# A two-layer decoder trunk on one core: work moved to GpSimd, and layer two's first key blocks begun on the first tokens

## The chip, the cores and the metric

The kernel runs on one core of a Trainium2 chip. Its engines are TensorE (PE in the profile; PEld is its weight load), VectorE (DVE), ScalarE (ACT), GpSimd (POOL) and SyncE (SP), which here only issues the transfers from memory. Every engine works through its own instructions in order, and they wait for each other with semaphores. The metric is the device time of one execution in microseconds (us), lower is better. 0.2% of it, about 1.25 us, is what a comparison of runs can tell from no change.

## What is computed

256 tokens of 1024 features pass two layers. Each layer has an attention part with two kinds of heads and a squared-ReLU MLP, and each part is wrapped in normalizations before and after.

```python
for l in range(DEPTH):                       # 2
    h = _rms_norm(x, g_pre_mix[l])
    parts = jnp.split(h @ w_in[l], split_at, axis=-1)
    o_nsa = _nsa_mixer(...)                  # 8 query heads, 2 key/value heads, head size 64
    o_fox = _fox_mixer(...)                  # 8 heads, forgetting attention
    mix = jnp.concatenate([o_nsa, o_fox], axis=-1) @ w_out[l]
    x = x + _rms_norm(mix, g_post_mix[l])
    h = _rms_norm(x, g_pre_mlp[l])
    y = jnp.square(jax.nn.relu(h @ w_up[l])) @ w_down[l]
    x = x + _rms_norm(y, g_post_mlp[l])
```

An NSA head has three branches, mixed with learned gates: attention over compressed blocks, over selected blocks, and over a window. With 256 tokens the selection takes every block and the window every earlier token, so branches 1 and 2 are two causal attentions over different keys and values. The compressed branch joins 32 tokens of keys (or values) into one vector, sends it through a small network with a GELU, and so gets 15 compressed keys and values. Keys and queries of the other branches are rotated by position (the first 16 of 64 features). A FoX head is causal attention with a bias from cumulated forget gates.

## The kernel before

**Numbers as pairs.** To reach float32 accuracy with TensorE's fast format, each operand is split into a high part (ACT copies it, rounded: `whi`, and the halves of `xT`, `qS`, `kx`, `oT`, `aT`) and the rest (DVE subtracts: `wlo`). Every product becomes three: high-high, high-low, low-high. So every weight tile costs one ACT and one DVE instruction, 1024 columns each (`Weights.get`, L621).

**Stages of a layer.** (1) The input projection. One chunk (chunk 1) has tokens as rows and holds the values and gates; 16 blocks of 128 columns have tokens as columns (`block`, L1225): 0 and 1 are the keys of branches 1 and 2 (`kT`), 2 and 3 the raw keys and values for compression (`cT`), 4 to 7 NSA queries, 8 to 15 FoX queries and keys. (2) Attention, spread over the rest of the projection, which fills PE between the small steps (`fill`, L1293). (3) The output projection, then `sandwich` (L856): normalize, add to x, and make the next transposed operand `xT`. (4) The MLP, eight chunks of `up` and `down`, then again `sandwich`.

**Turn into layer two.** In layer two chunk 1 goes token half by token half (`in_chunk` with `by_token`, L1127): all products for tokens 0 to 127, and only then those for 128 to 255, so that the first can run while the second half's `sandwich` is still at work. Its last steps (transposes into `xT`, then `m` and the update of x) are called inside that loop (L1445 to L1450). Then come blocks 0, 1, 2 and so on; each adds up in one of the two `acc` banks of PSUM over all 256 tokens: eight 512-column products with `whi` (high and low half of xT at once) and eight 256-column ones with `wlo`. The two `acc` banks first hold the MLP sums of the second token half, and `m` reads them last.

**Rotation.** `turned` (L972) multiplies by a sine table (`m`), shuffles partitions, multiplies the source by a cosine table (`y`), adds, and splits. It runs three times a layer: for the keys, and for two pairs of query blocks. The tables carry the row normalization (`row_scales`, L1249).

**Gather for compression.** `gather_blocks` (L982) lays the raw keys or values out for the compressing network in `kstk` and `kstv`: eight copies of 64 partitions x 120 elements each, from key head g and position parity j, and one copy of the position vector. Where g equals j the copy stays in its own partitions, otherwise it goes to the other half of them. For keys all eight are on ACT, for values all eight on DVE.

**One attention element.** There are 24 in a layer: NSA pair x parity x branch (16) and FoX pair x parity (8). Scores on PE; DVE adds the mask and takes the row minimum (`pr`, `st`); ACT takes the exponential with row sums; DVE the reciprocal; then `scale` (L1358) multiplies the two pieces of the probabilities (128 and 256 columns) by the reciprocal and the gate: NSA branch 1 on ACT, NSA branch 2 and FoX on DVE. PE then turns the three 128-column pieces (`probs_T`, L1374), ACT copies them out, and they are multiplied with the values later. The loop (L1483) scales element i-1 beside the scores of i, and turns i-2.

**Order.** The program first records every operation (`Recorder`), and then works out one fixed order for each engine (`order`, L483): it lays the operations out with a table of prices (`_cost`, L576, and `_latency`, L562), derives due times, and tries 140 slightly shifted rankings. So a change of a price or an engine changes the order everywhere, and PE's order on the chip is fixed. Before the change the recorder knows tensor, vector, scalar and sync; GpSimd has no part.

Of the kernel before, what the change touches and what calls it, by code (L numbers as in the profile page):

```python
# [24 lines left out]
P = 128  # L25
# [198 lines left out]
class Recorder:  # L224
    def __init__(self, nc, tc):
        self.nc, self.tc = nc, tc
        self.ops, self.fifo, self.key, self.hot, self.lane, self.group = [], {}, None, False, None, None
        self.after, self.cuts = None, []
        for e in ("tensor", "vector", "scalar", "sync"):
            setattr(self, e, _Engine(self, e))  # L230

    def tile(self, pool, shape, dtype, name, tag=None, bufs=1, psum=False):
# [69 lines left out]
    def schedule(self, rank):  # L302
# [9 lines left out]
        for op in self.ops:  # L312
            op.missing, op.ready, op.start = len(op.deps), 0.0, None
            for b in op.bufs:
                left[b] = b.ops
        waiting = {e: [] for e in ("tensor", "vector", "scalar", "sync")}
        busy = dict.fromkeys(waiting, 0.0)
        bus, last, sent = 0.0, None, 0
        busy["sync"] = 730.0
# [124 lines left out]
    def trial(self, out, seed):  # L444


        rng = np.random.default_rng(seed)
        late = rng.exponential(LATE[seed % 2], len(self.ops))
        ends, left = {}, {b: b.ops for q in self.fifo.values() for b in q}
        slots = {tag: [None] * q[0].bufs for tag, q in self.fifo.items()}  # L450
        free = dict(tensor=0.0, vector=0.0, scalar=0.0, sync=730.0)
        bus, last, sent, gone, reach = 0.0, None, 0, {}, [0.0] * (len(self.cuts) + 1)
        for n, op in enumerate(out):
            t = free[op.engine]
            for d, lat in op.deps.items():
                t = max(t, ends[d] + lat)
            for b in op.bufs:
                if left[b] == b.ops:
                    ring = slots[b.tag]
                    x, i = min((gone[p] if p else 0.0, i) for i, p in enumerate(ring) if p is None or not left[p])  # L460
                    ring[i] = b
                    t = max(t, x)
            if op.engine == "sync":
                free["sync"] = t + 470
                sent += 1
                bus = max(bus, t + 1150) + op.cost * (1.0 if t > CALM else EARLY) + (THIRD if sent == 3 else 0)
                ends[op] = bus + 900 + (late[n] if t > CALM else 0)
            else:
                ends[op] = t + op.cost
                if op.engine == "tensor":  # L470
                    ends[op] += _turn(last, op)
                    last = op
                    reach[op.stage] = max(reach[op.stage], ends[op])
                elif t > CALM:
                    ends[op] += FEW
                free[op.engine] = ends[op]
            for b in op.bufs:
                left[b] -= 1
                gone[b] = max(gone.get(b, 0.0), ends[op] + (260 if b.psum else 150))
        reach[-1] = max(ends.values())  # L480
        return np.diff([0.0] + reach)
# [80 lines left out]
def _latency(a, b):  # L562
    if a.engine == "sync":
        return 50.0
    if a.engine == b.engine == "tensor":
        return 0.0
    if a.engine == "tensor":
        return 40.0 + (360.0 if b.name == "tensor_tensor_reduce" else 200.0)
    if b.engine == "tensor":
        return 100.0 + (260.0 if a.engine == "vector" else 230.0)  # L570
    if a.engine == b.engine:
        return 190.0 if a.engine == "vector" else 225.0
    return 40.0 + (130.0 if a.engine == "vector" else 145.0)


def _cost(op, views):  # L576
    out = op.args[0] if op.args else op.kw["out"]
    n = int(np.prod(out.shape[1:]))
    if op.engine == "sync":
        v = views[0][1]  # L580
        return v.shape[0] * int(np.prod(v.shape[1:])) * 4 / 320.0
    if op.engine == "tensor":
        if op.name == "stretch":
            if op.args[2][0][0] == "transpose":
                return 108.0 * len(op.args[2])

            tiles = [_shape(x[1][1]) for x in op.args[2]]
            return sum((x[1][0].ix.size / (2.4 if x[1][1].dtype == F32R else 0.6) + 20) / (P // min(t))
                       for x, t in zip(op.args[2], tiles)) + RETILE * sum(a != b for a, b in zip(tiles, tiles[1:]))
        if op.name == "transpose":  # L590
            return 83.0 if op.args[1].dtype == F32R else 108.0
        if op.args[1].dtype == F32R:
            return 13.6 + n / 2.4
        return max(220.0, 3 + n / 0.6)
    if op.engine == "vector":
        if op.name == "reciprocal":
            return 60 + 6.5 * n
        if op.name == "tensor_reduce":
            n = int(np.prod(op.args[1].shape[1:]))
        fast = op.name in ("tensor_copy", "tensor_scalar", "memset") and not any(v.buf.psum for _, v in views)  # L600
        aps = sum(isinstance(v, View) for v in op.args[2:4]) if op.name == "tensor_scalar" else int(
            op.name == "scalar_tensor_tensor" and isinstance(op.args[2], View))
        return 68 + 64 * aps + n * (0.52 if fast else 1.04) + 10 * (op.name == "tensor_tensor_reduce")
    src = op.args[1]
    aps = sum(isinstance(op.kw.get(k), View) for k in ("bias", "scale", "accum_out"))
    return n / 1.2 + (55 if src.buf.psum else 92) + 93 * aps
# [54 lines left out]
def trunk(nc, A, consts_in, out, sbp, pp):  # L661
# [260 lines left out]
    for l in range(DEPTH):  # L922
# [49 lines left out]
        def turned(src, hi, lo):  # L972
# [2 lines left out]
            y = tokt("y").rearrange("p (b n) -> p b n", b=2)  # L975
            nc.vector.tensor_mul(m, src, two(T["rS"]))
            nc.vector.stream_shuffle(m, m, TURNED)
            nc.vector.tensor_mul(y, src, two(T["rC"]))
            nc.vector.tensor_add(y, y, m)
            split(y, (hi, lo))  # L980

        def gather_blocks(si):  # L982
# [4 lines left out]
            for g in range(2):  # L987
                rows = slice(g * HD, g * HD + HD)
                for j in range(2):
                    h = slice(j * HD, j * HD + HD)  # L990
                    for i in (0, 8):
                        o, x = kst[s][h, i:i + 8, g, 0:15], src[rows, :, i // 8:i // 8 + 15, j]
                        if si:
                            nc.vector.tensor_copy(o, x)
                        else:
                            nc.scalar.activation(o, x, AF.Copy)
            nc.vector.tensor_copy(kst[s][:, :, :, 15:16], posT[s][:, :, None, None].to_broadcast([P, 16, 2, 1]))

        def hidden_part(s, q):
            if q == 0:  # L1000
# [123 lines left out]
            T["cum"] = cum  # L1124


        def in_chunk(c, evac, by_token=False):  # L1127
            n = columns(l, c)[1] - columns(l, c)[0]
            parts = parts_of(l, c)
            begin = len(nc.ops)  # L1130
            ps = [None, None]
            ws = {}

            def piece(t, k, hi, lo, k0):
                if k == 0:
                    ps[t] = psum("os"[t] if first else "ox"[t] if by_token else "acc")
                mm3(ps[t][:, :n], [y[:, k, t * P:t * P + P] for y in xT[:2]], (hi[:, k - k0, :], lo[:, k - k0, :]),
                    k == 0, k == 7)

            if by_token:  # L1140
                for t in range(NT):
                    for q, (k0, k1) in enumerate(parts):
                        if t == 0:
                            ws[q] = weight(l, "in", c, q)
                        for k in range(k0, k1):
                            piece(t, k, *ws[q], k0)
                            yield
                    evac(t, ps[t])
                    yield
                return  # L1150
            for q, (k0, k1) in enumerate(parts):
                w = weight(l, "in", c, q)
                for k in range(k0, k1):
                    for t in range(NT):
                        piece(t, k, *w, k0)
                        yield
            nc.key = begin if EVKEY else None
            for t in range(NT):
                evac(t, ps[t])
            nc.key = None  # L1160
            yield

        def block_home(b):

# [108 lines left out]
        def stream():  # L1273
            def part(name, gen):
                yield from gen
                done.add(name)
            for b in range(4 if first else 0, NB):
                yield from part(b, block(b))
            yield from part("c5", in_chunk(5, evac5))
            for k in range(LASTK):  # L1280
# [77 lines left out]
        def scale(e, p, st):  # L1358
            kind, pair, par, br = e[:4]
            nc.vector.reciprocal(st[:, 2:4], st[:, 2:4])  # L1360
            for a, b, t in SEGS:
                if kind == "fox":
                    nc.vector.tensor_scalar(p[:, a:b], p[:, a:b], st[:, 2 + t:3 + t], None, op0=OP.mult)
                elif br == 1:
                    c = 3 * (2 * pair + par) + br
                    if t == 0:
# [1 line left out]
                    nc.scalar.activation(p[:, a:b], p[:, a:b], AF.Copy, scale=st[:, 2 + t:3 + t])  # L1368
                else:
                    c = 3 * (2 * pair + par) + br  # L1370
                    nc.vector.tensor_scalar(p[:, a:b], p[:, a:b], st[:, 2 + t:3 + t], gate[t][:, c:c + 1],
                                            op0=OP.mult, op1=OP.mult)

        def probs_T(*es):  # L1374
# [67 lines left out]
                        r_mix[t] = rstd_of_x(t, "rm")  # L1442
        else:

            for n, _ in enumerate(in_chunk(1, evac1, by_token=True)):  # L1445
                if n == 6:
                    urgent(carry)
                    next(carry)
# [1 line left out]
                        r_mix[t] = rstd_of_x(t, "rm")  # L1450
        if first:
            nc.scalar.activation(selr, cst[:, C_SEL:C_SEL + 8], AF.Copy)
        else:
            fill_to(1)
        row_scales()
        kx = [tile([P, 2, S], F32R, name="kx", tag=f"kx{j}") for j in range(2)]
        posT = {"k": rows[:, 0:16], "v": rows[:, 16:32]}
# [256 lines left out]
```

## Time and profile before

| | |
|---|---|
| time, median of 3 runs | 623.85 us (623.78 to 624.29) |
| the profiled execution, its own time | 623.83 us |
| its span, first to last instruction | 622.1 us |
| TensorE (PE) busy | 609.5 us, 98% |
| VectorE (DVE) busy | 475.0 us, 76% |
| ScalarE (ACT) busy | 389.9 us, 63% |
| GpSimd (POOL) busy | 0.2 us |

In the profile a row of a group names line, engine, operation, tiles (out<-in), shape and count, then busy time and the mean of one in ns, and after the second bar the idle time ahead and what ended it. Nearly all rows have line L535, the helper that emits the recorded operations, so they are told apart by tile and shape. A timeline row has start, length, engine and group, and in brackets the idle time before it. Matmuls overlap and their ends are modelled, so intervals from start to start say more than their lengths. A window row has busy time of PE, PEld, DVE, ACT and POOL in turn, then TensorE's clock, and the transfers.

### The profile page before, as it was taken

How to read it: one execution, taken by the hardware profiler on the slowest of the kernel's cores; microseconds unless marked ns; L12 is line 12 of the kernel's file. 1: busy time of each engine (PE TensorE's matmuls, PEld its weight loads, DVE VectorE, ACT ScalarE, POOL GpSimd, SP SyncE). 2: the span in 40 equal slices, each digit the busy share in tenths (PEclk: the TensorE clock that was granted, in tenths of full speed). 3: DMA queues.
4: the chain of work that ended last, by engine and by line, in shares of the span. 5: the costliest groups of instructions: out<-in, count | busy, mean ns of one | idle time of the engine just before them, and what ended most of it. 6: DMA issues, size and time to landing. Idle time of an engine off the chain costs nothing.

```text
span 622.1 us, 9781 instructions
## 1 busy us (share of the span) xinstructions
PE 609.5 (98%) x3472; PEld 505.2 (81%) x3472; DVE 475.0 (76%) x1057; ACT 389.9 (63%) x802; POOL 0.2 (0%) x4
## 2 busy tenths in 40 slices
PE   9999999999999999999999999999999999999995
PEld 8877777778888888888878778878888888888884
DVE  6889997789976566566599999996997666566544
ACT  6869796667655455455476588975766555556422
POOL 0000000000000000000000000000000000000000
PEclk9999999999999999999999999999999999999998
DMA  8967865219766556555427645552486556555101
GB/s 296 402 236 260 298 192 171 102 35 290 251 192 205 181 187 201 189 180 191 136 81 245 244 136 213 202 179 67 166 273 205 177 195 202 192 181 204 34 1 68
DMA packets 36353, 115.98 MB, mean 186 GB/s; under 512 B 4432, under 2 KB 6224, under 8 KB 36304
## 3 DMA queue, kind: packets, MB, share of 16 engines
q1 hardware_dynamic: 36304, 115.36, 54.7%
q8 instruction: 27, 0.44, 0.3%
q14 instruction: 22, 0.18, 0.1%
HBM read 114.30 MB, written 1.05 MB: 185 GB/s over the span
## 4 chain that ended last, share of the span: by engine, by line
PE 86%; DVE 8%; ACT 4%; issue 1%; DVEq 0%
PE s L535 34%; PE acc L535 25%; PE x L535 20%; PE o L535 7%; DVE wlo L535 2%; ACT pr L535 1%; DVE m L535 1%; ACT kstk L535 1%; ACT whi L535 1%; DVE y L535 1%; DVE pr L535 1%; DVE kstv L535 0%; DVE mg L535 0%; DVE qT L535 0%; ACT rl L535 0%
## 5 line engine op out<-in xcount | busy, mean ns | idle before, releaser
L535 DVE TENSOR_TENSOR wlo<-wraw,whi 128x1024 fp32r<-128x1024 f32 (+2 forms) x200 | 230.6, 1159 | 91.6 <-ACT whi L535 91.0
L535 ACT ACTIVATE whi<-wraw 128x1024 fp32r<-128x1024 f32 (+3 forms) x200 | 199.8, 1006 | 121.6 <-PE acc L535 58.6
L535 PE MATMUL s<-xT,whi 128*128 128x512 f32 x448 | 111.9, 392 | 0.0
L535 PEld LDWEIGHTS s<-xT,whi 128*128 128x128 f32 x448 | 81.4, 189 | 15.1
L535 PE MATMUL acc<-whi,aT 128*128 128x512 f32 x256 | 88.5, 390 | 0.0
L535 PE MATMUL x<-whi,aT 128*128 128x512 f32 x256 | 88.4, 390 | 0.0
L535 PE MATMUL acc<-xT,whi 128*128 128x512 f32 (+1 forms) x242 | 66.3, 400 | 0.3 <-DVE qT L535 0.3
L535 PEld LDWEIGHTS s<-xT,wlo 128*128 128x128 f32 x448 | 61.1, 190 | 4.4
L535 PE MATMUL s<-xT,wlo 128*128 128x256 f32 x448 | 62.5, 282 | 0.0
L535 ACT ACTIVATE pr<-pr,st 128x128 f32<-128x128 f32 (+1 forms) x128 | 55.1, 448 | 9.4 <-DVE st L535 9.3
L535 PEld LDWEIGHTS acc<-whi,aT 128*128 128x128 f32 x256 | 48.0, 188 | 10.0
L535 PEld LDWEIGHTS x<-whi,aT 128*128 128x128 f32 x256 | 48.1, 188 | 9.7
L535 PEld LDWEIGHTS acc<-xT,whi 128*128 128x128 f32 x242 | 43.1, 191 | 9.6 <-issue 1.1
L535 PE MATMUL x<-wlo,aT 128*128 128x512 f32 x128 | 50.0, 390 | 0.0
L535 PE MATMUL acc<-wlo,aT 128*128 128x512 f32 x128 | 49.9, 390 | 0.0
L535 PE MATMUL acc<-xT,wlo 128*128 128x256 f32 x240 | 37.1, 285 | 0.5 <-DVE wlo L535 0.5
L535 PEld LDWEIGHTS acc<-xT,wlo 128*128 128x128 f32 x240 | 33.6, 189 | 3.4 <-DVE wlo L535 0.9
L535 ACT ACTIVATE rl<-h 128x512 f32<-128x512 f32 x28 | 17.5, 624 | 18.7 <-DVE h L535 18.7
L535 PEld LDWEIGHTS acc<-wlo,aT 128*128 128x128 f32 x128 | 24.0, 188 | 4.9
L535 PEld LDWEIGHTS x<-wlo,aT 128*128 128x128 f32 x128 | 24.1, 188 | 4.5
L535 ACT ACTIVATE rl<-x 128x512 f32<-128x512 f32 x24 | 14.7, 612 | 20.1 <-PE x L535 16.0
L535 PE MATMUL o<-whi,xT 128*128 128x512 f32 (+1 forms) x80 | 26.1, 377 | 0.0
(224 smaller groups left out, 865.9 us busy)
## 6 DMA issues: line engine op xcount, KB each, us to landing
wraw<-in_w_up_dram SPq DMA_DIRECT2D x64, 512.0 KB, 4.2
wraw<-in_w_down_dram SPq DMA_DIRECT2D x64, 512.0 KB, 3.3
wraw<-in_w_fm_dram SPq DMA_DIRECT2D x28, 512.0 KB, 5.0
wraw<-in_w_out_dram SPq DMA_DIRECT2D x16, 512.0 KB, 6.6
wraw<-in_w_dram SPq DMA_DIRECT2D x9, 512.0 KB, 3.6
w<-in_cmp_w_k_dram SPq DMA_DIRECT2D x8, 512.0 KB, 5.6
w<-in_cmp_w_v_dram SPq DMA_DIRECT2D x8, 512.0 KB, 3.8
wraw<-in_w_dram SPq DMA_DIRECT2D x6, 256.0 KB, 4.2
```

The costliest lines, as they stand in the source:

```text
L535: getattr(getattr(self.nc, op.engine), name)(*[real(v) for v in args], **{k: real(v) for k, v in kw.items()})
```

## The change

- `scale`: the two multiplications of NSA branch 2 and of FoX go from DVE to GpSimd (64 instructions over both layers). NSA branch 1 stays on ACT.
- `gather_blocks`: copies with g equal to j (four of eight, "straight down" in their own partitions) go to GpSimd, the four others to ACT, for keys and values alike; the position copies go from DVE to GpSimd.
- `turned`: the multiplication with the cosine table goes from DVE to GpSimd.
- Layer two: a new generator `by_token` replaces the option of `in_chunk`. After the products of token half 0 it begins blocks 0 and 1 for those tokens (`half_block`, eight 256-column products with `whi` each), then does token half 1 of chunk 1, then the second halves of the two blocks and their `wlo` products. The stream of the other blocks starts at 2.
- The recorder and its layout get GpSimd as an engine, with prices of its own.

```diff
-        for e in ("tensor", "vector", "scalar", "sync"):
+        for e in ("tensor", "vector", "scalar", "gpsimd", "sync"):
...
+    if "gpsimd" in (a.engine, b.engine):
+        return 260.0
...
+    if op.engine == "gpsimd":
+        return 160 + n * (2.2 if op.name.startswith("tensor_tensor") or op.name == "tensor_mul" else 1.0)
...
             nc.vector.stream_shuffle(m, m, TURNED)
-            nc.vector.tensor_mul(y, src, two(T["rC"]))
+            nc.gpsimd.tensor_mul(y, src, two(T["rC"]))
...
-                        if si:
-                            nc.vector.tensor_copy(o, x)
+                        if g == j:
+                            nc.gpsimd.tensor_copy(o, x)
                         else:
                             nc.scalar.activation(o, x, AF.Copy)
-            nc.vector.tensor_copy(kst[s][:, :, :, 15:16], posT[s][:, :, None, None].to_broadcast([P, 16, 2, 1]))
+            nc.gpsimd.tensor_copy(kst[s][:, :, :, 15:16], posT[s][:, :, None, None].to_broadcast([P, 16, 2, 1]))
...
+        def by_token():
+            n = columns(l, 1)[1] - columns(l, 1)[0]
+            ws, wb, pb, homes = {}, {}, {}, {}
+
+            def tokens(t):
+                ps = psum("ox"[t])
+                for q, (k0, k1) in enumerate(parts_of(l, 1)):
+                    if t == 0:
+                        ws[q] = weight(l, "in", 1, q)
+                    for k in range(k0, k1):
+                        piece(t, k, ps[:, :n], *ws[q], k0)
+                        yield
+                evac1(t, ps)
+                yield
+
+            def half_block(b, t):
+                o = pb[b].rearrange("p (j n) -> p j n", j=2)[:, :, t * P:t * P + P]
+                for k in range(8):
+                    nc.tensor.matmul(o, wb[b][0][:, k, :], xT[2][:, k, :, t * P:t * P + P], start=t == 0 and k == 0,
+                                     stop=False, skip_group_check=True)
+                    if k % 2:
+                        yield
+
+            yield from tokens(0)
+            for b in range(2):
+                homes[b] = block_home(b)
+                wb[b] = weight(l, "in", "b", b)
+                pb[b] = psum("acc")
+                yield from half_block(b, 0)
+            yield from tokens(1)
+            for b in range(2):
+                yield from half_block(b, 1)
+                for k in range(8):
+                    nc.tensor.matmul(pb[b][:, S:], wb[b][1][:, k, :], xT[0][:, k, :], start=False, stop=k == 7,
+                                     skip_group_check=True)
+                    if k % 2:
+                        yield
+                both_halves(homes[b], pb[b])
+                yield
...
-            for b in range(4 if first else 0, NB):
+            for b in range(4 if first else 2, NB):
...
                 if kind == "fox":
-                    nc.vector.tensor_scalar(p[:, a:b], p[:, a:b], st[:, 2 + t:3 + t], None, op0=OP.mult)
+                    nc.gpsimd.tensor_scalar(p[:, a:b], p[:, a:b], st[:, 2 + t:3 + t], None, op0=OP.mult)
...
-                    nc.vector.tensor_scalar(p[:, a:b], p[:, a:b], st[:, 2 + t:3 + t], gate[t][:, c:c + 1],
+                    nc.gpsimd.tensor_scalar(p[:, a:b], p[:, a:b], st[:, 2 + t:3 + t], gate[t][:, c:c + 1],
                                             op0=OP.mult, op1=OP.mult)
...
-            for n, _ in enumerate(in_chunk(1, evac1, by_token=True)):
+            for n, _ in enumerate(by_token()):
...
-        else:
-            fill_to(1)
         row_scales()
```

More of the change, by code (lines that the diff above doesn't have):

```diff
@@ L315, in schedule @@
                 left[b] = b.ops
-        waiting = {e: [] for e in ("tensor", "vector", "scalar", "sync")}
+        waiting = {e: [] for e in ("tensor", "vector", "scalar", "gpsimd", "sync")}
         busy = dict.fromkeys(waiting, 0.0)
@@ L450, in trial @@
         slots = {tag: [None] * q[0].bufs for tag, q in self.fifo.items()}
-        free = dict(tensor=0.0, vector=0.0, scalar=0.0, sync=730.0)
+        free = dict(tensor=0.0, vector=0.0, scalar=0.0, gpsimd=0.0, sync=730.0)
         bus, last, sent, gone, reach = 0.0, None, 0, {}, [0.0] * (len(self.cuts) + 1)
@@ L1124, in forget_sums, with in_chunk @@
             T["cum"] = cum
-        def in_chunk(c, evac, by_token=False):
+        def in_chunk(c, evac):
             n = columns(l, c)[1] - columns(l, c)[0]
-            parts = parts_of(l, c)
             begin = len(nc.ops)
             ps = [None, None]
[L1132 to L1151, printed above, removed]
+            for q, (k0, k1) in enumerate(parts_of(l, c)):
                 w = weight(l, "in", c, q)
@@ L1154, in in_chunk @@
                     for t in range(NT):
-                        piece(t, k, *w, k0)
+                        if k == 0:
+                            ps[t] = psum("os"[t] if first else "acc")
+                        piece(t, k, ps[t][:, :n], *w, k0)
                         yield
@@ L1161, in in_chunk, with piece @@
             yield
+        def piece(t, k, ps, hi, lo, k0):
+            mm3(ps, [y[:, k, t * P:t * P + P] for y in xT[:2]], (hi[:, k - k0, :], lo[:, k - k0, :]), k == 0, k == 7)
+        def by_token():
[34 more added lines that the diff above has]
+                yield
         def block_home(b):
```

## The prediction

> **What bounds the kernel now.** I read the page's busy times first, then what TensorE (PE) waited for, then the groups of the other engines, and last the timeline at the places where PE waits.
>
> ```profile
> span 622.1 us, 9781 instructions
> PE 609.5 (98%) x3472; PEld 505.2 (81%) x3472; DVE 475.0 (76%) x1057; ACT 389.9 (63%) x802; POOL 0.2 (0%) x4
> ```
>
> PE is busy for 609.5 of 622.1 us, so no edit that leaves PE's work alone can win more than the 12.6 us between them, and GpSimd (POOL) does next to nothing. The profiled execution took 623.83 us, 1.73 us more than its span; the median of the three timed runs is 623.85 us, so sums made against 623.83 hold for the median too.
>
> What PE waited for, as total, times and longest:
>
> ```profile
> PE s L535 <- ACT pr L535: 1.3, 1, 1.3
> PE acc L535 <- DVE wlo L535: 0.5, 1, 0.5
> PE s L535 <- DVE hs L535: 0.4, 1, 0.4
> PE s L535 <- DVE hv L535: 0.4, 1, 0.4
> PE acc L535 <- DVE qT L535: 0.3, 1, 0.3
> PE s L535 <- DVE pcT L535: 0.3, 1, 0.3
> ```
>
> These six single waits, 3.2 us together, all lie in the attention stages, and all are for work that the diff thins out. The rest of PE's idle time is at the start, at the turns between stages and at the end; of these the diff touches only the turn into layer two. So the reachable gain is small: these 3.2 us, and stretches where PE counts as busy but its starts are late.
>
> **What moves to GpSimd, and the prices before.** From the groups that keep shapes apart (busy, mean ns):
>
> ```profile
> L535 DVE TENSOR_SCALAR pr<-pr,st,gate 128x256 f32<-128x256 f32 x16 | 6.5, 404 | 0.0
> L535 DVE TENSOR_SCALAR pr<-pr,st 128x256 f32<-128x256 f32 x16 | 5.5, 349 | 0.2
> L535 DVE TENSOR_SCALAR pr<-pr,st,gate 128x128 f32<-128x128 f32 x16 | 5.4, 338 | 0.0
> L535 DVE TENSOR_SCALAR pr<-pr,st 128x128 f32<-128x128 f32 x16 | 4.4, 280 | 0.0
> L535 DVE COPY kstv<-cT 64x120 f32<-64x120 f32 x16 | 4.1, 258 | 0.2
> L535 ACT ACTIVATE kstk<-cT 64x120 f32<-64x120 f32 x16 | 6.6, 413 | 3.8 <-DVE cT L535 3.6
> L535 DVE TENSOR_TENSOR y<-qT,rCS 128x512 f32<-128x512 f32 x4 | 2.7, 679 | 0.0
> L535 DVE TENSOR_TENSOR y<-kT,rCS 128x512 f32<-128x512 f32 x2 | 1.4, 687 | 0.0
> L1704 POOL MEMSET const-float32-0.0<- 128x1 f32 x1 | 0.1, 98 | 0.2 <-issue 0.2
> ```
>
> VectorE (DVE) loses 21.8 us of scaling (64 instructions), 4.1 us of gathering and 4.1 us of cosine products: 30 of 475 us, about 15 per layer. ScalarE (ACT) keeps its 16 gathers, but as four for k and four for v per layer where it had eight for k. GpSimd has no row for any of this; a one-column fill took 98 ns there. For a pair of scales (128 and 256 columns) the lower bound is DVE's own price, 338 + 404 = 742 ns gated or 629 ns not. For the upper I take the ratio that ACT shows for the same copy, 413/258 = 1.6, which makes 1.19 us, plus one foreign instruction waited out. GpSimd issues no DMA, and only its four fills stand in its queue, so nothing is pushed back behind what moves there.
>
> **Term 1, layer one's first blocks: -1.4 us.**
>
> ```profile
> 39.78 3.39 ACT L535 ACTIVATE kstk<-cT 64x120 f32<-64x120 f32 x8 [3.57 <-DVE cT L535]
> 43.61 0.42 DVE L535 TENSOR_TENSOR rl<-acc,rl 128x256 f32<-128x256 f32 x1 [1.59 <-ACT rl L535]
> 44.79 0.39 ACT L535 ACTIVATE pr<-pr,st 128x128 f32<-128x128 f32 x1
> 49.09 0.88 PE L535 MATMUL s<-cst,pr 128*128 128x128 f32 x6 [1.34 <-ACT pr L535]
> ```
>
> Eight gathers hold ACT for 3.39 us; behind them wait an evacuation that DVE stands idle for (1.59 us) and the first exponentials. PE then loses 1.34 us before the first transposes. With four gathers ACT is free 1.7 us earlier, more than the 1.34. Two cosine products leave the DVE stretch just ahead (2 x 0.68), where PE waits 0.5 and 0.3 us for wlo and qT. Bounds: all of it, -2.1 (1.34 + 0.5 + 0.3), and 0, if ACT's next work (the weight splits) sets the same time. I take -1.4, the wait that has one plain cause.
>
> **Term 2, the same place in layer two: -0.5 us.**
>
> ```profile
> 351.06 1.05 DVE L535 COPY kstv<-cT 64x120 f32<-64x120 f32 x4
> 353.17 0.51 ACT L535 ACTIVATE pr<-pr,st 128x256 f32<-128x256 f32 x1 [4.78 <-DVE st L535]
> 350.00:360.00 10.00, 9.38 (x58) 7.24 (x55) 9.77 (x48) 6.83 (x25) 0.00 (x0) 1.00 0.79 313
> ```
>
> Here DVE is the late one: its copies (8 x 258 ns = 2.1 us) run before the score minima, for which ACT idles 4.78 us. PE idles 0.62 us in this window (10 - 9.38). Bounds -0.6 to +0.5 (if the copies, slower on GpSimd, make the v blocks late instead); I take -0.5.
>
> **Term 3, small DVE waits: -0.3 us.** The rows hv and pcT above, 0.7 us in both, stand behind a full DVE. Its relief takes part of it: -0.7 to 0, half taken.
>
> **Term 4, layer two's start by tokens: -0.6 us.** The start times of PE, and what DVE and ACT do there:
>
> ```profile
> 312.01 0.39 PE L535 MATMUL o<-whi,xT 128*128 128x512 f32 x1
> 317.45 1.44 PE L535 MATMUL s<-cst,mg 128*128 128x128 f32 x8
> 319.71 0.73 PE L535 MATMUL x<-whi,xT 128*128 128x512 f32 x2 [0.19 <-DVE xT L535]
> 324.83 1.98 PE L535 MATMUL acc<-xT,whi 128*128 128x512 f32 x8
> 326.64 1.11 PE L535 MATMUL acc<-xT,wlo 128*128 128x256 f32 x8
> 327.59 2.00 PE L535 MATMUL acc<-xT,whi 128*128 128x512 f32 x8
> 434.29 1.04 PE L535 MATMUL s<-cst,mg 128*128 128x128 f32 x8
> 435.09 0.49 PE L535 MATMUL acc<-whi,oT 128*128 128x512 f32 x1
> 318.31 0.75 DVE L535 SCALAR_TENSOR_TENSOR m<-acc,r,gains 128x512 f32<-128x512 f32 x1
> 320.17 0.74 DVE L535 SCALAR_TENSOR_TENSOR m<-acc,r,gains 128x512 f32<-128x512 f32 x1
> 318.13 0.60 ACT L535 ACTIVATE xT<-s 128x512 fp32r<-128x512 f32 x1 [2.63 <-PE s L535]
> ```
>
> Token half 0 takes 312.01 to 317.45, 5.44 us for 24 products without a hitch. The eight transposes and the same 24 products for half 1 take 317.45 to 324.83, 7.38 us. Eight such transposes elsewhere take 0.80 us (434.29 to 435.09), so 7.38 - 5.44 - 0.80 = 1.14 us are waits, although the view lists 0.19 of them. The change puts two half blocks into this gap. They cost: eight 512-column products take 1.81 us (324.83 to 326.64), and the sixteen 256-column ones that replace them 2 x 0.95 (326.64 to 327.59), so +0.09 per block, +0.18 for two. Best case -0.96. Against it: both half blocks accumulate in "acc", whose two banks hold the last layer's sums until the two instructions m<-acc have read them, at 319.06 and 320.91, later than PE wants the first one (317.45). m needs neither the transposes nor the normalizing factor, so it can go earlier, at the price of 0.66 us or so on the mg products ahead of the transposes. The worst case is that both stay where they are, some +0.9. The hi splits fit: ACT idles 2.63 us there. I take -0.6.
>
> **Term 5, the cosine product itself: 0.** On the way to the first scores DVE has the sine product and its shuffle to do meanwhile, some 1.3 us, which cover 679 ns on GpSimd even at 1.6 times the price. Without that cover (the two products one after the other) it is +0.6 for each of the two that precede first scores, +1.2.
>
> **Term 6, scaled probabilities that come late: +0.6 us.** PE's order is fixed, so a pair of scales that comes after the time for which the order was laid out stops PE at the transposes, and all products queued behind. What the order allows now:
>
> ```profile
> 387.68 0.66 DVE L535 TENSOR_SCALAR pr<-pr,st,gate 128x128 f32<-128x128 f32 x2
> 388.54 0.88 PE L535 MATMUL s<-cst,pr 128*128 128x128 f32 x6
> 404.05 0.55 DVE L535 TENSOR_SCALAR pr<-pr,st 128x256 f32<-128x256 f32 x2
> 407.51 0.55 PE L535 MATMUL s<-cst,pr 128*128 128x128 f32 x3
> 40.00:120.00 80.00, 24.41 (x21) 1.00 0.62 211
> ```
>
> The first two rows leave 0.2 us between scale and transposes, the next two 2.9 us: some pairs are tight, some loose. I count half of the 32 pairs as tight, as an estimate. The new order is laid out with prices for GpSimd (160 ns plus 1.0 ns a column, 260 ns for each hand-over); with those no pair is late. Bounds 0 and the third case below, +5.9; I take +0.6, nearer 0, because loose pairs cost nothing and a stop of PE also lets the next pair catch up.
>
> **Sum:** -1.4 - 0.5 - 0.3 - 0.6 + 0 + 0.6 = -2.2 us; 623.83 - 2.2 = **621.6 us**.
>
> **The rivals.** *The two engines exclude each other (slower).* The last row above is DVE's wlo alone, the difference of two SBUF operands, between 40 and 120 us: 24.41 of 80 us, 31%. If a GpSimd instruction cannot run beside it, it waits on average 0.31 x half of 1.2 us = 0.19 us, a pair 0.37 us, which the order does not know. Sixteen tight pairs make +5.9 in place of +0.6: 623.83 - 2.8 + 5.9 = 626.9 us. It decides from 2.8/16 = 0.18 us of lateness per tight pair. For it speaks that DVE is 97.7% busy in the window shown for layer two; against it that no row of POOL work shows any such wait. The Trainium skill states this rule (SBUF — State Buffer, § Who interferes with whom): a DVE instruction with two SBUF inputs and a GpSimd instruction that reads SBUF share a read interface, and the second fully blocks. No row here shows it. The skill's GPSIMD Engine Reference, § 4.1 Engine selection, adds that two-input work is about 2x slower there and one-input work roughly line rate; by that the cosine product would take some 1.4 us as an estimate and its cover would just fail, +0.1 each.
>
> *The gains do not reach PE (no change).* The whole order is laid out anew, and what DVE and ACT are freed from is filled with weight splits, so PE waits elsewhere for as long: terms 1 to 3 shrink to a fourth (-0.55), term 4 to 0, and term 6 stays: 623.9 us. For it speaks that the six waits have five different causes; against it that term 1 has one cause, which goes.
>
> *Only the start by tokens fails.* The banks come late, term 4 is +0.9: 623.83 - 2.2 + 0.6 + 0.9 = 623.1 us, no change either.
>
> **How the numbers follow.** My forecast has 0.52, its own range 619.5 to 622.5; exclusion 0.23; no gain 0.17; the failed start 0.08. About 0.2% (1.25 us) is what a measurement of this kernel can tell from no change. So faster is 0.52, within 0.2% is 0.25, slower is 0.23. The range goes down to 619.0 (terms 1 to 4 at their best, -2.1 - 0.6 - 0.7 - 0.96 = -4.4, nothing late: 619.5, and a little for waits hidden as in term 4) and up to 627.5, past the exclusion case.
>
> **What would show it.** Right: ACT's run of k gathers at some 1.7 us, and no wait of PE for pr near 49 us; the stretch from the last product of token half 0 to the end of half 1 without 1.1 us of late starts; the first exponentials of layer two sooner after the scores. Wrong: PE waits for POOL pr, POOL instructions well over the prices above, or wlo stretched beyond 1.22 us while POOL runs; PE waiting for acc's banks near 318 us. If PE's waits in the attention stages add up to more than the 3.2 us, the forecast is wrong.

## The result and the profile after

The changed kernel takes 628.38 us (627.78 to 629.12) against 623.91 us (623.78 to 624.29): a ratio of 1.0071, 95% interval 1.0054 to 1.0089. It is slower by 4.5 us, where 2.2 us less was forecast. The profiled execution took 628.2 us. One of the ten executions of e1 below, 1009.88 us at a mean granted clock of 0.56, is left out of its median.

The page's first lines, and then what PE waited for (total, times, longest), both of the changed kernel:

```profile
span 626.4 us, 9901 instructions
...
PE 608.8 (97%) x3488; PEld 504.6 (81%) x3488; DVE 457.9 (73%) x967; ACT 390.7 (62%) x802; POOL 78.6 (13%) x94
```

```profile
PE s L535 <- POOL pr L535: 4.9, 6, 1.2
PE acc L535 <- DVE qT L535: 2.0, 1, 2.0
...
PE acc L535 <- ACT whi L535: 0.8, 1, 0.8
PE s L535 <- ACT pr L535: 0.5, 1, 0.5
```

DVE is relieved of 17 us (475.0 to 457.9), not of the 30 that the prediction added up, in part because its sine products got longer (last row below). GpSimd spends 78.6 on what it got, and PE is as busy as before; only its waits grew. The 4.9 us for scaled probabilities and the 2.0 us for `qT` did not exist, or were 0.3 us, before. The groups of GpSimd, and the sine product of DVE, with shapes kept apart (busy, mean ns, idle before):

```profile
L535 POOL TENSOR_SCALAR pr<-pr,st 128x256 f32<-128x256 f32 x16 | 17.6, 1106 | 9.5 <-DVE st L535 6.0 <-PE acc L535 3.5
L535 POOL TENSOR_SCALAR pr<-pr,st,gate 128x256 f32<-128x256 f32 x16 | 15.1, 944 | 41.0 <-DVE st L535 37.5 <-ACT whi L535 3.5
L535 POOL TENSOR_SCALAR pr<-pr,st 128x128 f32<-128x128 f32 x16 | 13.1, 822 | 12.8 <-DVE st L535 12.8
L535 POOL TENSOR_SCALAR pr<-pr,st,gate 128x128 f32<-128x128 f32 x16 | 10.9, 683 | 21.0 <-DVE st L535 18.5 <-PE s L535 2.5
L535 POOL TENSOR_TENSOR y<-qT,rCS 128x512 f32<-128x512 f32 x4 | 6.7, 1664 | 6.2 <-DVE qT L535 6.2
...
L535 DVE TENSOR_TENSOR m<-qT,rCS 128x512 f32<-128x512 f32 x4 | 4.9, 1214 | 0.0
```

A FoX scale (`pr<-pr,st`, one factor) takes longer than a gated one (two factors), on the same shape. A FoX pair takes 822 + 1106 ns = 1.93 us; the order was laid out for 288 + 416 = 0.70 us.

Where the time went is seen in windows over the FoX stages of the two layers. The columns are busy us of PE, PEld, DVE, ACT and POOL, then the clock, DMA share and GB/s. First before, then after:

```profile
95.00:146.00 51.00, 50.36 (x303) 37.81 (x302) 41.01 (x109) 32.82 (x81) 0.00 (x0) 1.00 0.37 119
399.00:453.00 54.00, 54.00 (x329) 42.73 (x326) 45.39 (x112) 37.74 (x84) 0.00 (x0) 1.00 0.41 138
```

```profile
95.00:146.00 51.00, 48.85 (x295) 35.92 (x294) 33.05 (x84) 31.56 (x76) 14.89 (x18) 1.00 0.31 99
399.00:453.00 54.00, 51.73 (x315) 39.53 (x315) 37.03 (x90) 37.08 (x85) 17.38 (x18) 1.00 0.34 110
```

DVE has 8 us less to do in each, and PE idles 2.15 and 2.27 us where it idled 0.64 and none. One such place, from the timeline after:

```profile
404.10 5.59 POOL L535 TENSOR_SCALAR pr<-pr,st 128x256 f32<-128x256 f32 x4 [3.40 <-DVE st L535]
...
405.58 3.72 DVE L535 TENSOR_TENSOR wlo<-wraw,whi 128x1024 fp32r<-128x1024 f32 x3 [0.78 <-ACT whi L535]
...
409.97 0.31 PEld L535 LDWEIGHTS s<-cst,pr 128*128 128x128 f32 x3 [0.56 <-POOL pr L535]
```

Four scales stand beside three subtractions of `wlo` and need 5.59 us; the transposes wait for the last of them.

Stage lengths, from the starts of PE's rows in the timelines (us; "FoX" runs from the first FoX scores, their bias product `s<-cum,selr`, to the MLP's first product, "turn" from layer two's first product to its first scores):

| profiled run | first scores at | first scores to transposes | FoX, layer one | turn | FoX, layer two |
|---|---|---|---|---|---|
| before | 37.24 | 11.85 | 49.55 | 37.44 | 50.75 |
| after | 37.80 | 10.19 | 51.73 | 36.56 | 54.13 |
| FoX scales back on DVE (e1) | 40.13 | 9.63 | 49.87 | 36.56 | 50.98 |
| start by tokens alone (e3) | 36.87 | 11.84 | 49.59 | 36.73 | 49.27 |
| gathers alone (e14) | 37.12 | 10.94 | 49.50 | 37.30 | 52.75 |

The FoX stages gave +2.2 and +3.4 us, more than the whole loss; the turn and the stretch after the first scores did win. Borders shift where the order is another (gathers alone have 52.75 us in the last column and are the shortest as a whole), so columns compare best within one order: the rows of after and e1.

### The profile page after: what moved, and what is told of

Its sections match the earlier page's. It is cut to its first block, busy times and chain, and to the rows that moved or that the text cites. A ratio compares the mean times of both kernels' runs of the same rounds, so it can differ in the third digit from the quotient of the medians.

```text
span 626.4 us, 9901 instructions
## 1 busy us (share of the span) xinstructions
PE 608.8 (97%) x3488; PEld 504.6 (81%) x3488; DVE 457.9 (73%) x967; ACT 390.7 (62%) x802; POOL 78.6 (13%) x94
## 4 chain that ended last, share of the span: by engine, by line
PE 82%; DVE 7%; ACT 5%; issue 2%; POOL 2%; DMA 1%; POOLq 0%; DVEq 0%; ACTq 0%
PE s L535 33%; PE acc L535 24%; PE x L535 18%; PE o L535 7%; POOL pr L535 2%; DVE wlo L535 2%; ACT whi L535 1%; ACT pr L535 1%; DVE m L535 1%; DMA wraw<-in_w_fm_dram 1%; DVE pr L535 1%; ACT rl L535 1%; ACT kstk L535 0%; DMA wraw<-in_w_dram 0%; POOLq L1737 0%
## 5 line engine op out<-in xcount | busy, mean ns | idle before, releaser
L535 ACT ACTIVATE pr<-pr,st 128x256 f32<-128x256 f32 (+1 forms) x128 | 55.3, 448 | 5.7 <-DVE st L535 5.4
L535 POOL TENSOR_TENSOR y<-kT,rCS 128x512 f32<-128x512 f32 x2 | 5.0, 2483 | 239.9 <-DVE rCS L535 239.9
L535 POOL TENSOR_SCALAR pr<-pr,st,gate 128x256 f32<-128x256 f32 (+1 forms) x32 | 25.7, 814 | 62.0 <-DVE st L535 56.0
L535 POOL TENSOR_SCALAR pr<-pr,st 128x128 f32<-128x128 f32 (+1 forms) x32 | 30.3, 964 | 22.3 <-DVE st L535 18.8
L535 PE MATMUL s<-cst,pr 128*128 128x128 f32 x144 | 24.3, 281 | 5.5 <-POOL pr L535 4.9
```

Of the source, the lines that this page charges most:

```text
L535: getattr(getattr(self.nc, op.engine), name)(*[real(v) for v in args], **{k: real(v) for k, v in kw.items()})
```

## The experiments

Times are medians; the kernel before took 623.68 to 623.91 us beside each set.

**m1: the prices by themselves.** A small kernel with none of the trunk's computation: scales, copies and products of the shapes at issue on each engine alone, then six GpSimd scales (three with one factor, three with two) beside a run of one kind of DVE work.

> This kernel computes nothing of the trunk: it only runs the GpSimd instructions of the change on tiles of their own, in stretches: DVE alone, GpSimd alone, then three one-factor and three two-factor scalings of 128x256 beside one kind of DVE instruction each (SBUF minus SBUF 1024 columns, SBUF times SBUF 512, PSUM plus SBUF 256, one-input scaling 512, copy 1024), beside ACT copies, and two 512-column products on both engines. If GpSimd's own price is the cause, it needs about 0.60 and 0.92 us for a one-factor scaling of 128 and 256 columns alone, 0.46 and 0.56 for a two-factor one, and the same beside DVE. If the two engines exclude each other, the six scalings, 4.4 us alone, take 7 us and more beside DVE instructions with two SBUF inputs (up to one 1.2 us instruction each), DVE's own instructions there get longer too, and nothing changes beside PSUM plus SBUF and beside ACT.

The timeline (alone; beside `wlo`, both operands in SBUF; beside an addition with one operand in PSUM; beside a scaling with one input; beside a copy):

```profile
14.02 3.73 DVE L43 TENSOR_TENSOR wlo<-wraw,whi 128x1024 fp32r<-128x1024 f32 x3
...
25.79 1.30 POOL L38 TENSOR_SCALAR pr<-pr,gate 128x128 f32<-128x128 f32 x2
...
28.96 1.94 POOL L38 TENSOR_SCALAR pr<-pr,gate 128x256 f32<-128x256 f32 x2
30.89 1.20 POOL L41 TENSOR_SCALAR prb<-prb,gate,gate 128x256 f32<-128x256 f32 x2
...
38.52 3.22 POOL L38 TENSOR_SCALAR pr<-pr,gate 128x512 f32<-128x512 f32 x2
41.73 1.63 POOL L41 TENSOR_SCALAR prb<-prb,gate,gate 128x512 f32<-128x512 f32 x2
...
49.71 13.67 DVE L43 TENSOR_TENSOR wlo<-wraw,whi 128x1024 fp32r<-128x1024 f32 x10
...
53.95 1.88 POOL L38 TENSOR_SCALAR pr<-pr,gate 128x256 f32<-128x256 f32 x1
55.82 1.06 POOL L41 TENSOR_SCALAR prb<-prb,gate,gate 128x256 f32<-128x256 f32 x1
...
79.93 0.92 POOL L38 TENSOR_SCALAR pr<-pr,gate 128x256 f32<-128x256 f32 x1
80.84 0.54 POOL L41 TENSOR_SCALAR prb<-prb,gate,gate 128x256 f32<-128x256 f32 x1
...
92.34 1.16 POOL L38 TENSOR_SCALAR pr<-pr,gate 128x256 f32<-128x256 f32 x1
...
107.12 1.69 POOL L38 TENSOR_SCALAR pr<-pr,gate 128x256 f32<-128x256 f32 x1
```

Two things add up. With one factor a scale costs 0.65 and 0.97 us alone (1.30 / 2, 1.94 / 2), where the order was laid out for 0.29 and 0.42; with two factors 256 columns cost 0.60. And DVE holds GpSimd up: beside the addition from PSUM, where nothing is lost, the two forms take 0.92 and 0.54 us, beside `wlo` 1.88 and 1.06, while `wlo` goes from 1.24 to a mean of 1.37 us. The Trainium skill's rule (SBUF — State Buffer, § Who interferes with whom) fits these rows in which instructions get in each other's way, also in that a copy and a one-input scaling on DVE can hold GpSimd up (1.69 and 1.16 us). That each stands still for the whole of the other's instruction is not what the rows show: from 50.96 to 59.79 us, in 8.8 us, pass all six scales (4.4 us undisturbed) and six whole subtractions (7.3 us at the 1.22 us of one alone). In the changed kernel `wlo` hardly suffers (1226 ns in the mean, 1220 before).

**e1: FoX scales back on DVE, the order kept.**

```diff
             for op in self.order():
+                if op.engine == "gpsimd" and op.name == "tensor_scalar" and op.args[3] is None:
+                    op.engine = "vector"
```

> The changed kernel with its order of instructions kept word for word; only the FoX scalings are issued by DVE, at the same places. If GpSimd's FoX scalings are what costs the time (by price or by exclusion), the FoX stages lose the 2.2 and 4.3 us that they gained: about 622 us, under the kernel before. If the new order itself is worse, it stays at 626 us or above.

623.70 us, ratio 1.0000 (0.9988 to 1.0012): 4.7 us less than the changed kernel, its whole loss, and the FoX stages are back at 49.87 and 50.98 us. But 32 instructions fewer for GpSimd did not bring the gain forecast for the rest. PE's waits, and windows behind the longest of them:

```profile
PE acc L537 <- DVE qT L537: 2.0, 1, 2.0
PE s L537 <- POOL pr L537: 1.2, 1, 1.2
```

```profile
34.00:38.00 4.00, 2.02 (x12) 1.68 (x11) 4.00 (x10) 1.51 (x3) 0.00 (x0) 0.91 0.75 302
38.00:42.00 4.00, 4.00 (x20) 2.60 (x19) 2.81 (x7) 1.86 (x6) 1.43 (x4) 0.66 0.35 112
```

The wait for `qT` stays, and in this profile the granted clock falls to 0.66 behind it, which moves the first scores from 37.80 to 40.13 us.

**e2: FoX scales on GpSimd in the form with two factors.**

```diff
-  nc.gpsimd.tensor_scalar(p[:, a:b], p[:, a:b], st[:, 2 + t:3 + t], None, op0=OP.mult)
+  nc.gpsimd.tensor_scalar(p[:, a:b], p[:, a:b], st[:, 2 + t:3 + t], 1.0, op0=OP.mult, op1=OP.mult)
```

> The changed kernel with the same order; the FoX scalings stay on GpSimd but in the two-factor form (second factor 1.0), which takes 1.01 us a pair in the profile in place of 1.53 when nothing disturbs it. If GpSimd's own price in that form is the cause, 16 pairs a half of them tight make some -4 us: about 624.5. If waiting for DVE is the cause, the pair still waits and it stays within 1 us of 628.4.

624.99 us, ratio 1.0012 (1.0002 to 1.0023). The groups and the wait:

```profile
L535 POOL TENSOR_SCALAR pr<-pr,st 128x128 f32<-128x128 f32 x16 | 9.0, 563 | 16.1 <-DVE st L535 16.1
L535 POOL TENSOR_SCALAR pr<-pr,st 128x256 f32<-128x256 f32 x16 | 8.4, 527 | 15.0 <-DVE st L535 10.5 <-PE acc L535 3.8 <-PE s L535 0.5
```

```profile
PE s L535 <- POOL pr L535: 1.6, 2, 1.0
```

A multiplication by 1.0 that computes nothing wins 3.4 us (628.38 - 624.99), because it selects a form that takes 1.09 us a pair in place of 1.93. So of the FoX scales' 4.7 us some 3.4 are the form's own price, and 1.3 (624.99 - 623.70) what is left, hand-over and DVE's hindrance by the look of it; no run parts these two. The split is loose, because the clock plays into it: three of e2's executions, with a mean granted clock of 0.996 to 0.998, took 623.25 to 623.66 us, the other seven, at 0.993 to 0.995, 624.68 to 625.64. By those three the form is nearly the whole.

**e3 and e13: the start by tokens alone,** everything else as before, with two seeds of the order search.

> The kernel before with only the start of layer two by tokens; GpSimd does nothing. If that part works as in the profile of the changed kernel (0.9 us less in the turn), about 623.0 us. If laying the order out anew costs or wins by itself as much as the parts do, it can lie anywhere within 2 us of 623.9.

> The start by tokens alone with the other seed. The kernel before took 623.9 and 622.9 us with the two seeds. Theory A (the start by tokens gives 0.7 to 0.9 us, which the stage from layer two's first product to its first scores shows in each run): 621.9 to 622.4 us. Rival B (its 0.9 us with the first seed were the draw): 622.7 to 624 us.

622.86 us both times (ratios 0.9985, 0.9976 to 0.9995, and 0.9982, 0.9973 to 0.9991). What that is worth depends on e8.

**e8 and e9: before and after with the other seed.**

```diff
-        rng = np.random.default_rng(1)
+        rng = np.random.default_rng(2)
```

> The kernel before with one number changed: the seed from which the search over instruction orders draws its delays, so that the order is chosen afresh and nothing else differs. This measures what laying the order out anew is worth by chance. Theory A (the other runs' differences are those of their edits): within 0.5 us of the kernel before, 623.3 to 624.4 us. Rival B (a new order by itself moves the time by 1 to 3 us, so that a gain of 2 to 3 us proves nothing of the edit): outside that.

> The changed kernel with the other seed of the order search. Theory A (the scales and products on GpSimd cost their 4 to 5 us in any order that does not know of the exclusion): 627 to 630 us. Rival B (the order that was drawn is unlucky): 624 us or less.

Before: 622.87 us, ratio 0.9981 (0.9972 to 0.9990), 1.0 us less for nothing but another seed. After: 630.77 us, ratio 1.0108 (1.0092 to 1.0123). So the loss is not one unlucky order (4.5 and 7.9 us against before with the same seed), but an edit that lays the order out anew is known to 1 us or so at best, and the changed kernel itself moved by 2.4 us. The start by tokens gains 0.8 us with the first seed (against the 623.68 beside it) and nothing with the second.

**e14 and e15: the gathers alone,** on the kernel before, with both seeds. **e5 and e10: gathers and start by tokens.**

> The kernel before with the gather straight down by GpSimd and nothing else of the change, first seed. Theory A (terms 1 and 2 are right in size, 1.9 us): 621.5 to 622.4 us. Rival B (the gathers give nothing by themselves): 623.3 to 624.3 us.

> The same with the second seed, against 622.9 us of the kernel before with that seed. Theory A: 620.5 to 621.5 us. Rival B: 622.3 to 623.3 us.

> The changed kernel with both kinds of scales and the cosine products back on DVE, its order laid out anew: only the gather straight down by GpSimd and the start by tokens are left of the change. Against the kernel with only the start by tokens (622.86 us) this measures terms 1 and 2 of the prediction. Theory A (the gather gives 1.4 us in layer one and 0.5 us in layer two when no scale or product is in its way): 621.0 us, and TensorE does not wait for pr before layer one's first transposes. Rival B (the gather only moves the wait, something else ends at the same time): 622.5 to 623.2 us.

> Gathers and start by tokens alone (620.5 us) with the other seed of the order search. Theory A (terms 1 and 2, the gathers, are worth the 2.4 us that lie between that kernel and the one with the start by tokens alone): 620 to 621.2 us. Rival B (part of the 2.4 us is the luck of the draw): 621.5 to 623 us.

| | first seed | second seed |
|---|---|---|
| before | 623.91 | 622.87 |
| gathers alone | 620.59 | 620.31 |
| gathers and start by tokens | 620.50 | 619.73 |

Ratios to before with the first seed: 0.9950 (0.9936 to 0.9963), 0.9945 (0.9933 to 0.9958), 0.9944 (0.9932 to 0.9956), 0.9931 (0.9919 to 0.9944). The gathers win 3.3 and 2.6 us, the start by tokens 0.1 and 0.6 on top; the last entry is the fastest kernel of this study. Rows of e14's timeline:

```profile
38.21 1.45 ACT L535 ACTIVATE kstk<-cT 64x120 f32<-64x120 f32 x4 [2.31 <-DVE cT L535]
...
48.06 0.82 PE L535 MATMUL s<-cst,pr 128*128 128x128 f32 x6
...
350.36 0.51 ACT L535 ACTIVATE pr<-pr,st 128x256 f32<-128x256 f32 x1 [0.70 <-DVE st L535]
```

ACT's k gathers take 1.45 us (3.39 before), the first transposes start at 48.06 without a wait (49.09 with 1.34), and layer two's exponentials wait 0.70 us for the row minima (4.78).

**e4 and e12: more work back on DVE in the changed kernel's order:** FoX scales and cosine products (e4), and the gated scales as well (e12). The edit is that of e1 with the other operations named.

> The changed kernel's list of instructions with every FoX scale and every cosine product issued by DVE at the same places of the list; the gathers, the gated scales and the start by tokens stay as the change has them. Theory A (the cosine product on GpSimd is what holds TensorE for 2.0 us before layer one's first scores, and that pause is what lets the clock fall to 0.66): the pause falls to the 0.3 to 0.5 us that the kernel before has there, the granted clock stays at 1.00 between 34 and 42 us, and the time is 623.83 less 1.5 to 2.5, 621.3 to 622.3 us. Rival B (the pause comes from the new order, in which the first key blocks stand otherwise, and the product's engine matters little): pause and clock stay, 623.5 to 624.2 us.

> The changed kernel's list of instructions with FoX scales, cosine products and gated scales all issued by DVE at the same places of the list; only the gathers stay on GpSimd. Against the run with FoX scales and products swapped (622.59 us) it gives the price of the 32 gated scales at one order. Theory A (they cost by exclusion, as the run laid out anew said, 1.7 us): 620.5 to 621.3 us. Rival B (in this order they are loose, and the 1.7 us were the draw): 622.2 to 623.2 us, as DVE gets 12 us of work more.

e4: 622.59 us, ratio 0.9980 (0.9972 to 0.9989), 1.1 us less than e1 and between its two theories. Two rows of e4:

```profile
PE acc L537 <- DVE qT L537: 1.0, 1, 1.0
...
L537 DVE TENSOR_TENSOR m<-qT,rCS 128x512 f32<-128x512 f32 x4 | 2.7, 668 | 0.0
```

The sine product is back at 0.67 us, half of the 2.0 us wait is gone, and the clock stays at 1.00. The other 1.0 us is there with gathers alone too (1.1 us in e14), so it does not come from the product; no run parts the gathers from the orders laid out for them. e12: 625.02 us (1.0022, 1.0011 to 1.0032), more than e4 by 2.4 and outside both expectations. PE now waits 0.8 us each for DVE's `pcT` and `gh`, which e4's list does not have: an order that was laid out without the gated scales on DVE seems to have no room for them there. With the order kept, giving work back can thus be worth more than it shows; e1 and e4 may have understated their gains.

**e7 and e11: gated scales, or cosine products, on top of gathers and start by tokens,** laid out anew.

> The gathers, the gated scales (two factors) and the start by tokens as in the change; FoX scales and cosine products on DVE; laid out anew with the measured prices of gathers and gated scales. Theory A (the gated scales are harmless on GpSimd, and free DVE of 6 us per layer that it has no use for): within 0.5 us of the kernel with gathers and start by tokens alone, 620.7 to 621.7 us. Rival B (they cost by exclusion like the FoX scales, though their stage is looser): 0.8 to 2 us more than that kernel.

> Gathers, start by tokens and the cosine products on GpSimd, both kinds of scales on DVE, laid out anew. Against gathers and start by tokens alone (620.5 us) this measures term 5. Theory A (sine and cosine product shut each other out, so that the sine product takes 1.8 us where it took 0.7): 1.0 to 2.0 us more, 621.5 to 622.5 us. Rival B (the prediction's 0): 620.2 to 620.8 us.

e7: 622.18 us (0.9973, 0.9963 to 0.9983), 1.7 more than e5; it was also laid out with the measured prices of gathers and gated scales. e11: 622.59 us (0.9978, 0.9969 to 0.9988), 2.1 more. Each is past what a new seed did to e5 (0.8 us), but neither was run with the second seed, and the changed kernel moved by 2.4. For e11 the trace speaks too: its sine products take 1209 ns and the 2.0 us wait for `qT` is there. For e7 it is the time alone, and e12 points the other way.

**e6: the whole change, laid out with the prices of GpSimd alone.**

```diff
-        return 160 + n * (2.2 if ... else 1.0)
+        if op.name == "tensor_mul":
+            return 1290.0
+        if op.name == "tensor_scalar":
+            return 286 + 2.48 * n if op.args[3] is None else 352 + 0.8 * n
+        return 385.0 if n > 32 else 240.0
```

> The whole change, but its order is laid out with the GpSimd prices that were measured alone (one factor 0.60 and 0.92 us, two factors 0.45 and 0.56 us, cosine product 1.29 us, gathers 0.39 us) in place of 160 ns plus 1.0 or 2.2 ns a column. Theory A (the loss comes from instructions that cost more than the order was laid out for, alone): the order makes room, the FoX stages fall back from 51.7 and 54.1 us to about 50 and 51, and the time is 623.5 to 624.5 us. Rival B (the loss comes from the two engines shutting each other out, which no fixed price tells the order): most of it stays, 626 to 628 us.

630.10 us (626.70 to 631.29), ratio 1.0093 (1.0074 to 1.0111). By the median right prices cure nothing, though PE's wait for late probabilities falls from 4.9 to 2.1 us. But the run is no clean answer, as its windows in layer two show:

```profile
350.00:352.00 2.00, 0.80 (x5) 0.23 (x3) 2.00 (x2) 1.58 (x4) 1.96 (x3) 1.00 0.93 367
352.00:354.00 2.00, 1.55 (x10) 0.87 (x10) 2.00 (x8) 0.52 (x4) 1.36 (x3) 0.75 0.98 375
354.00:356.00 2.00, 2.00 (x9) 1.79 (x8) 1.99 (x15) 1.83 (x8) 0.00 (x0) 0.50 1.01 412
...
358.00:360.00 2.00, 2.00 (x7) 1.58 (x6) 1.32 (x5) 1.74 (x7) 0.47 (x2) 0.54 0.01 2
```

Behind another pause, PE's 1.65 us wait for `qS`, the clock loses up to half its rate for some 8 us. The executions show the price: the one with a mean granted clock of 0.998 took 626.70 us, the five at 0.988 to 0.991 took 629.07 to 631.29. By that single execution, with the clock kept, this kernel stands in the 626 to 628 us of its second theory.

## Why the prediction was wrong

- **Term 6 (late scaled probabilities, +0.6) failed.** FoX scales alone cost 4.7 us (e1), gated ones perhaps 1.7 (e7, which e12 does not bear out). The sign of being wrong that the prediction named is there: PE waits 4.9 us for `POOL pr`. The step that failed reads "with those no pair is late": it took the prices of the layout, which the diff brought along, for the chip's. A FoX pair costs 0.92 us more than laid out when nothing disturbs it (0.65 + 0.97 against 0.70), and 0.31 more in the kernel (1.93 - 1.62). The upper bound for a pair, 1.19 us and a foreign instruction waited out, did cover 1.93 us; the value that I took into the sum lay at the other end, because the layout's prices seemed to decide between the two.
- **Term 5 (cosine product, 0) failed.** The cover (sine product and shuffle, "some 1.3 us") assumed that the two products run together at DVE's usual price. Each of them reads two operands in SBUF, and they hold each other up. The sine product's row before, then rows of the changed kernel:

```profile
L535 DVE TENSOR_TENSOR m<-qT,rCS 128x512 f32<-128x512 f32 x4 | 2.7, 668 | 0.0
```

```profile
30.61 2.20 POOL L535 TENSOR_TENSOR y<-qT,rCS 128x512 f32<-128x512 f32 x1 [0.17 <-DVE qT L535]
...
31.58 1.78 DVE L535 TENSOR_TENSOR m<-qT,rCS 128x512 f32<-128x512 f32 x1
...
36.22 1.65 PE L535 MATMUL acc<-xT,whi 128*128 128x512 f32 x6 [1.98 <-DVE qT L535]
```

  The sine product takes 1.78 in place of 0.67 us (in m1 1.63 in place of 0.69, beside GpSimd's products), and DVE, full here, is late with `qT` for PE. It costs 1.1 (order kept) to 2.1 us (laid out anew); the +1.2 of the bound is inside by luck, for another reason than the one it was given for.
- **Terms 1 and 2 (gathers, -1.9) were right in mechanism and too small:** -3.3 and -2.6 by themselves. By stages of e14, 2.0 us are won before layer one's first FoX scores and 1.3 between layer two's first scores and its MLP. In the changed kernel the first transposes do come sooner (10.19 us after the scores), but the next ones already wait for GpSimd:

```profile
49.76 0.44 PE L535 MATMUL s<-cst,pr 128*128 128x128 f32 x2 [1.25 <-POOL pr L535]
```

- **Term 4 (start by tokens, -0.6): the mechanism held.** Rows after, from the transposes to the first full block:

```profile
319.34 1.03 PE L535 MATMUL s<-cst,mg 128*128 128x128 f32 x8
320.13 2.16 PE L535 MATMUL acc<-xT,whi 128*128 128x256 f32 x16
322.13 0.40 PE L535 MATMUL x<-whi,xT 128*128 128x512 f32 x1
...
327.59 1.12 PE L535 MATMUL acc<-xT,whi 128*128 128x256 f32 x8
```

  0.79 + 2.00 + 5.46 us without a late start, and the banks of "acc" were free in time. The size is 0.1 to 0.8 us by the draw, once nothing; -0.6 cannot be told from that.
- **Term 3 (small waits, -0.3)** was not tested by itself. Its two rows, hv and pcT, are gone from the changed kernel's list of waits.
- **The rivals.** Exclusion, 626.9 us, named the right place, and its +5.9 us for late pairs stands beside 4.7 + 1.7 = 6.4 measured. That is in part luck: its price per pair, 0.37 us, is under a third of what a FoX pair lost (1.93 - 0.70 = 1.23 us); the form's own price is the larger part, and no view of the kernel before could show it. The 1.5 us from there to 628.38 are about the size of term 5. "Gains do not reach PE" was wrong, the gathers' did; "only the start by tokens fails" too.

In a sum: gathers -2.9 and start by tokens -0.3 (means over the two seeds), gated scales +1.7, cosine products +2.1, all by orders laid out anew, and FoX scales +4.7 with the order kept: +5.3 us, against the +4.5 measured (+7.9 with the other seed). The parts come from different orders, so that they nearly add up is no proof of each, the gated scales' least of all. What the second seed adds is not explained.

## What to carry to other kernels

Before work goes to an engine that has no row in the profile, measure the very forms of instruction there, alone and beside what its neighbour runs at that time; with guessed prices in the layout each late result stops TensorE, and the prices measured alone did not cure it either (e6). Relief counts where engines wait for the relieved one (the gathers, -2.9 us), not by its amount (22 us of scaling taken off DVE, +6.4 us). And where every edit lays the order out anew, measure what another seed does first, since no comparison of such edits resolves less.

## What the runs showed of the hardware that was not expected

- **One factor is dearer than two on GpSimd.** From 128 to 512 columns a scale with one factor goes from 0.65 to 1.61 us, 2.5 ns a column; with two factors 512 columns cost 0.82 us and 256 cost 0.60, 0.8 ns a column. The Trainium skill (GPSIMD Engine Reference, § 4.1 Engine selection) calls one-input work roughly line rate; of the two forms only the second bears it out.
- **Short pauses can lower the clock.** Of six profiles with PE's 2.0 us wait before layer one's first scores, three show 0.64 to 0.69 of the clock in the 4 us behind it (e1, e2, e11) and three do not; the 1.65 us in e6 brought 0.50 in layer two. Other waits of 1.0 to 1.5 us did not (1.1 in e14, 1.5 in e7 and e9). So a pause of this length can do it and need not; what decides is not shown. The Trainium skill (TensorE: Matmul & The Clock Gate, § Why this matters for your kernels) warns of gaps above some 3 us; here less was enough.
